# A two-layer hybrid diffusion backbone on one core: an output projection split into two passes, a product loop turned inside out, and tiles moved to other start addresses

## The chip, the cores and the metric

One core of a Trainium2 chip runs the whole program. The metric is device time in microseconds (us), lower is better; three runs of the kernel before are given, and a fourth execution was taken by the hardware profiler. All times below are from those.

## The reference, cut to what matters

```python
def diff_attend(q, k, v, lam):                       # layer 1, 8 heads of two 64-wide halves
    s = jnp.einsum('bqhd,bkhd->bhqk', q, k) * DIFF_SUB_DIM ** -0.5
    p = softmax(s).reshape(b, DIFF_HEADS, 2, lq, k.shape[1])
    a = p[:, :, 0] - lam * p[:, :, 1]
    return jnp.einsum('bhqk,bkhd->bqhd', a, v)
def finish(o):                                       # per-head RMS norm, then the output projection
    o = rms_norm(o, subln_w) * (1.0 - lam_init)
    return o.reshape(..., 8 * 128) @ w_out
x = layer_norm(ALPHA * x + gate * finish(o))         # then the feed-forward part
...
def neighbourhood_attention(...):                    # layer 0: local keys plus context keys, one softmax
    return einsum(p_loc, v_r) + einsum(p_ctx, v_ctx)
def conv_ffn(u, w_up, conv_w, conv_b, w_down):
    val, gate = split(dwconv_centred(u @ w_up, conv_w, conv_b), 2)
    return (silu(gate) * val) @ w_down
```

There are 512 latent and 256 context tokens, width 1024, feed-forward width 2816. Layer 0 has a state-space branch beside neighbourhood attention, layer 1 the differential attention, and each layer ends in a feed-forward part. All data are float32.

## The kernel before, in words

**Precision.** Dense products run in fp32r on pairs: each operand is split into hi and lo, and `PASS` (hi x hi, hi x lo, lo x hi) makes three matmuls of what is mathematically one. `wchunk` (L127) loads 128x1024 of weights into `raw` by SP's queue, optionally multiplies by a gate row on POOL (L146), makes `whi` on ACT (L147) and `wlo` on DVE or POOL (L148). There are two `raw` buffers and eight `w` buffers.

**Where tiles lie.** Left-hand pools follow one another: `cst` (L84) ends at byte 22,080 of a partition, which is 64 past a multiple of 128, and the buffers of `blk`, `rawp`, `arp` and `wf` behind it are multiples of 128 bytes long, so all of them start 64 past one. `blk` holds activations (`u`, `ux`, `dact`, `act`, residual rows `y`) and `wf` the weight pairs. Right-hand pools hang from byte 229,344, 96 past a multiple of 128: the feed-forward activations `fact`, the split attention outputs `att` and the neighbourhood tiles (`nQ`, `nKh`, `V`) start 96 past one. In the pool `dp` of the differential attention, `K`, `Qh` and `Ql` happen to start at multiples of 128.

**Order.** The program is written in source order; a planner at build time (L1440, with a timeline of its own) gives each engine and each DMA queue one fixed order, with source order as priority and its own estimate of when operands are ready. On the chip each queue runs in that order and waits at its head.

**Neighbourhood attention** (`na_unit`, L723): a unit handles 128 queries and two heads, e = 0 and 1. Scores go to PSUM, softmax to `P`, TensorE transposes `P`, `Pt` is the copy of it in SBUF (L759), and then the value products (L765 to L767) run over e outside and over key chunks inside: the head e uses columns 64e to 64e+63 of the array and the same partitions of the PSUM tile `av`. Four pairs of heads have four units with four chunks and two context units with two chunks each. These products are plain fp32, and each shows as two records in the trace. `run` (L801) interleaves these units with the state-space groups and dense products.

**Feed-forward** (`up` L994, `down` L1019): `fpx` (512 latent tokens) and `fpc` (context) have `whi`/`wlo` as stationary operand and `u` as moving one, at L300; `pdn` at L1032 has a 128-token slice of `fact` as stationary operand and 512 columns of the weight as moving one.

**Differential attention** (L1201 to L1325). For a head `d_qk` makes rotated keys and queries; `d_head` (L1201) runs four rounds of 128 queries: scores `dSp` (L1210), maximum, exponential (L1217), difference `dP` (L1222), six transposes `atp` (L1227), value products `avp` (L1231), copy to `ob` and sum of squares (L1233, L1234). After each round it takes one step of a generator `filler`. Heads 0 to 5 are stored to DRAM (`scrO`). `d_prep` (L1242) takes two heads: a Sqrt on ACT for the norm, `ob` loaded back by SP (L1257), scaled (L1258), transposed through PSUM (`otp`, L1262), and split into `dact` (L1263, L1264). `d_out` (L1268) loads the projection weights of its heads, and for each of four token tiles tt and two column halves sums 3 products per head in one PSUM tile of the ring `pmm` (two slots) and adds the sum to `Yt[tt]` on DVE (L330).

Heads 0 and 1 are projected as filler of head 6, heads 2 and 3 as filler of head 7, and heads 4 to 7 after head 7 in one `d_out` of 12 products per sum, whose sums are followed by layer norm (`bn_stats`, `ln_to_u` L344: normalise, transpose `lntp`, scale, split into `u5`) and, on POOL, `affine` (L372).

PSUM is full: `pm2` two slots (tag mm), `pax` two (tag ax, used by `atp`, `avp`), `pS` two of double size (tag S, for scores).

Of the kernel before, what the change touches and what calls it, by code (L numbers as in the profile page):

```python
# [74 lines left out]
def emit(tc, T):  # L75
# [8 lines left out]
    cst = enter(tc.tile_pool(name="cst", bufs=1))  # L84
    blk = enter(tc.tile_pool(name="blk", bufs=18))
# [637 lines left out]
    def na_unit(Q, Kh, Kl, V, qo, k0, chunks, bias, out, pool, tp_, nb):  # L723
# [39 lines left out]
        for e in range(2):  # L763
            hp = HALF[e]
            for i, c in enumerate(chunks):  # L765
                m = toks[c][1]
                nc.tensor.matmul(av[hp], V[0:m, c, hp], Ss[e][1][0:m, i], start=(i == 0), stop=(i == len(chunks) - 1))  # L767
# [209 lines left out]
    def ffn(l, u, Y, with_ctx, u_next, last, close, pieces=()):  # L977
# [4 lines left out]
        fcw = fR.tile([128, 2 * NF, 4], F32, name="fcw")  # L982
# [259 lines left out]
    def d_prep(h, obs=None):  # L1242
        r = rso[:, h:h + 2].rearrange("p a b -> p (a b)")
        s0 = ds0[:, h:h + 2].rearrange("p a b -> p (a b)")
        nc.vector.tensor_scalar(r, dss[:, h:h + 2].rearrange("p a b -> p (a b)"), 1.0 / 128, None, op0=OP.mult)
# [6 lines left out]
        for i in range(2):  # L1252
            if obs:
                ob = obs[i]
            else:
                ob = (blk if h else dp).tile([128, 4, 128], F32, name="ob", tag="b" if h else "ob", bufs=None if h else 3)
                nc.sync.dma_start(ob, scrO[h + i])  # L1257
            (nc.gpsimd if h + i in OB_POOL else nc.vector).tensor_tensor(ob, ob, rso[:, h + i].unsqueeze(2).to_broadcast([128, 4, 128]), op=OP.mult)  # L1258
            at_ = blk.tile([128, 2, 512], F32R, name="dact", tag="b")
            tp = (pax if h == 6 else pmm).tile([128, 512], F32, name="otp", tag="ax" if h == 6 else "mm")  # L1260
            for q in range(4):
                nc.tensor.transpose(tp[:, 128 * q:128 * q + 128], ob[:, q], ident)  # L1262
            nc.scalar.activation(at_[:, 0], tp, AF.Copy, scale=sublnw)  # L1263
            nc.vector.scalar_tensor_tensor(at_[:, 1], tp, sublnw, at_[:, 0].bitcast(F32), op0=OP.mult, op1=OP.subtract)  # L1264
            acts.append(at_)
        return acts

    def d_out(hs, acts, wr=W, last=False):  # L1268
# [3 lines left out]
        n = 3 * len(hs)  # L1272
        for tt in range(4):
            bs = new_stats(dp) if last else None
            for hf in range(2):
                ps = pmm.tile([128, 512], F32, name="dpo", tag="mm")
                m = 0
                for kt in range(len(hs)):
                    for wi, ui in PASS:
                        nc.tensor.matmul(ps, acts[kt][:, ui, 128 * tt:128 * tt + 128], ws[kt][wi][:, 0, 512 * hf:512 * hf + 512],  # L1280
                                         start=(m == 0), stop=(m == n - 1))
                        m += 1
                add_ps(Yt[tt], ps, 512 * hf, 512, bs[:, hf] if last else None)
            if last:
                ln_to_u(Yt[tt], bs, tt, u5, sc3, sh3, dp, pS, "S", "dP", 4, 2)
            yield
# [3 lines left out]
    obs = []  # L1290
    filler, acts = (), []
    for h in range(8):
# [4 lines left out]
        obs = obs[-1:] + [d_head(h, *qk, Vh, filler)]  # L1297
# [5 lines left out]
        if h == 6:  # L1303
            qn = qx
# [4 lines left out]
        if h == 2:  # L1309
            acts = d_prep(0)  # L1310
        if h == 5:
            filler = d_out((0, 1), acts)
        if h == 6:
            acts = d_prep(2)
            filler = d_out((2, 3), acts, (blk, "b"))
        if h == 7:
            acts = d_prep(4)
# [4 lines left out]
    for _ in d_out((4, 5, 6, 7), acts + d_prep(6, obs), W, True):  # L1322
        pass
# [120 lines left out]
```

## Time and profile before

| what | us |
|---|---|
| runs | 2042.38, 2033.87, 2041.36 (median 2041.36) |
| profiled execution, its own time | 2034.78 |
| its span, first to last instruction | 2033.0 |
| PE busy | 1937.5 (95%) |
| weight loads (PEld) | 1649.1 (81%) |
| DVE, ACT, POOL busy | 1383.6, 893.9, 752.2 |

The profiled execution is 6.6 us below the median of the runs and within their spread. A row of the profile gives a group of instructions by line, engine and tiles (out<-in), their number, the time in which any of them ran, the mean of one, and the idle time of the engine before them with what ended it. Matmuls are pipelined: the duration of one (some 0.39 us for 512 columns) overlaps the next, and the cost in a stream is the distance from start to start. In a timeline row, consecutive instructions of one group are merged (x2), so the distance of two rows is to be divided by the number in the first.

### The profile page before, as it was taken

To read this page: it belongs to the slowest core of one execution; us is meant where nothing else is said; L and a number is where in the kernel's file an instruction comes from. 1 tells how busy PE (TensorE), PEld (TensorE's weight loads), DVE (VectorE), ACT (ScalarE), POOL (GpSimd) and SP (SyncE) were. 2 spreads that over 40 slices of the span, in tenths; PEclk is the share of its full clock that TensorE was granted. 3 is DMA by queue.
4 is the path that set the end of the run, shared out by engine and by line. 5 is a ranking of instruction groups with operands and counts; after the bars stand their busy time and mean duration, and the time that the engine had idled before them with its cause. 6 is when DMAs were issued, how large, how long until landed. Compare 5 with 4: busy or idle time off the path is not lost. (4 is left out here: it accounts for less than half of the span.)

```text
span 2033.0 us, 31103 instructions
## 1 busy us (share of the span) xinstructions
PE 1937.5 (95%) x11928; PEld 1649.1 (81%) x11928; DVE 1383.6 (68%) x2202; ACT 893.9 (44%) x1756; POOL 752.2 (37%) x635
## 2 busy tenths in 40 slices
PE   7998999999999889999999999999999899999998
PEld 5887878897677788888888887898997688888886
DVE  3757566767567968978776658676665776655567
ACT  3545456675343532222222233556564544333332
POOL 2136225245226835344444428421124274222123
PEclk9999999999899999999999999999999999999999
DMA  9335332233422234334333331422112223322231
GB/s 312 121 105 172 99 123 89 81 131 122 148 93 84 96 114 135 124 113 138 116 124 103 104 104 42 138 64 74 63 55 65 88 77 112 104 87 100 89 108 62
DMA packets 109299, 217.58 MB, mean 107 GB/s; under 512 B 27096, under 2 KB 45888, under 8 KB 109152
## 3 DMA queue, kind: packets, MB, share of 16 engines
q1 hardware_dynamic: 98480, 189.44, 28.7%
q0 software_dynamic: 6016, 20.03, 2.9%
q10 hardware_dynamic: 4656, 6.13, 1.0%
q8 instruction: 94, 1.54, 0.3%
q14 instruction: 53, 0.43, 0.1%
HBM read 202.81 MB, written 8.55 MB: 104 GB/s over the span
## 5 line engine op out<-in xcount | busy, mean ns | idle before, releaser
L147 ACT ACTIVATE whi<-raw 128x1024 fp32r<-128x1024 f32 (+1 forms) x205 | 215.3, 1056 | 410.2 <-PE fpc L300 143.3
L148 DVE TENSOR_TENSOR wlo<-raw,whi 128x1024 fp32r<-128x1024 f32 (+1 forms) x192 | 258.2, 1349 | 159.1 <-ACT whi L147 156.1
L324 POOL TENSOR_TENSOR y<-y,ev 128x512 f32<-128x512 f32 x144 | 210.0, 1479 | 206.8 <-DVE ev L322 165.2
L1032 PE MATMUL pdn<-whi,fact 128*128 128x512 f32 x880 | 277.8, 397 | 3.3 <-DVE ev L322 2.3
L300 PE MATMUL fpx<-ux,whi 128*128 128x512 f32 (+1 forms) x832 | 232.3, 364 | 2.1 <-DVE cv L991 2.1
L300 PE MATMUL fpx<-u,whi 128*128 128x512 f32 (+1 forms) x832 | 227.7, 359 | 2.8 <-DVE cv L991 1.8
L1032 PEld LDWEIGHTS pdn<-whi,fact 128*128 128x128 f32 x880 | 163.1, 188 | 42.6 <-DVE ev L322 4.0
L1016 POOL TENSOR_TENSOR fact<-cv,fact 128x768 fp32r<-128x768 f32 (+1 forms) x44 | 73.9, 1679 | 269.1 <-ACT fact L1015 269.1
L1032 PE MATMUL pdn<-wlo,fact 128*128 128x512 f32 x440 | 172.3, 394 | 0.0
L300 PEld LDWEIGHTS fpx<-ux,whi 128*128 128x128 f32 x832 | 150.1, 193 | 25.8 <-issue 3.9
L300 PEld LDWEIGHTS fpx<-u,whi 128*128 128x128 f32 x832 | 149.3, 191 | 26.7 <-ACT cv L987 2.0
L300 PE MATMUL fpx<-ux,wlo 128*128 128x512 f32 (+1 forms) x416 | 151.7, 365 | 1.8 <-DVE wlo L148 1.8
L300 PE MATMUL fpx<-u,wlo 128*128 128x512 f32 (+1 forms) x416 | 149.3, 360 | 1.3 <-DVE wlo L148 1.3
L300 PE MATMUL px<-ux,whi 128*128 128x512 f32 x448 | 149.8, 406 | 0.7 <-ACT whi L147 0.7
L991 DVE SCALAR_TENSOR_TENSOR cv<-fpx,fcw,cv 128x511 f32<-128x511 f32 x176 | 130.5, 744 | 28.2 <-ACT cv L987 26.9
L193 DVE SCALAR_TENSOR_TENSOR acc<-araw,condp,acc 128x512 f32<-128x512 f32 x140 | 131.1, 958 | 22.9 <-DMA araw<-in_ada_w 22.4
L146 POOL TENSOR_TENSOR raw<-raw,G 128x1024 f32<-128x1024 f32 x30 | 73.9, 2467 | 176.0 <-DMA raw<-in_w_down 94.4
L300 PE MATMUL fpc<-uc,whi 128*128 128x256 f32 x704 | 130.3, 283 | 1.4 <-DVE uc L370 1.4
L300 PEld LDWEIGHTS fpc<-uc,whi 128*128 128x128 f32 x704 | 111.9, 191 | 6.0 <-DVE uc L370 1.6
L375 POOL TENSOR_TENSOR y<-y,gb 128x256 f32<-128x256 f32 x112 | 101.4, 940 | 32.0 <-PE lntp L354 32.0
L322 DVE SCALAR_TENSOR_TENSOR ev<-pdn,G 128x512 f32<-128x512 f32 x120 | 81.1, 681 | 32.0 <-POOL y L324 17.9
L987 ACT ACTIVATE cv<-fpx,fcw 128x512 f32<-128x512 f32 x88 | 67.6, 770 | 79.7 <-PE fpx L300 77.4
(330 smaller groups left out, 4632.5 us busy)
## 6 DMA issues: line engine op xcount, KB each, us to landing
araw<-in_ada_w SPq DMA_DIRECT2D x96, 512.0 KB
raw<-in_w_up SPq DMA_DIRECT2D x88, 512.0 KB
raw<-in_w_down SPq DMA_DIRECT2D x44, 512.0 KB
E<-scr POOLq DMA_DIRECT2D x24, 512.0 KB, 5.0
raw<-in_w_dqk SPq DMA_DIRECT2D x16, 512.0 KB
raw<-in_w_qkv SPq DMA_DIRECT2D x12, 512.0 KB
raw<-in_w_out SPq DMA_DIRECT2D x12, 512.0 KB
raw<-in_w_bc SPq DMA_DIRECT2D x8, 512.0 KB
```

The source lines that it names most:

```text
L146: nc.gpsimd.tensor_tensor(raw, raw, gate, op=OP.mult)
L147: nc.scalar.activation(hi[:, :n], raw[:, :n], AF.Copy)
L148: (eng or nc.vector).tensor_tensor(lo[:, :n], raw[:, :n], hi[:, :n].bitcast(F32), op=OP.subtract)
L193: nc.vector.scalar_tensor_tensor(acc[:, s], raw[:, i], cs, acc[:, s], op0=OP.mult, op1=OP.add)
L300: nc.tensor.matmul(ps, w[wi][:, kc], rhs(kc, ui), start=(i == 0), stop=(i == n - 1))
L322: nc.vector.scalar_tensor_tensor(t, ps, r, Gh, op0=OP.mult, op1=OP.mult)
L324: eng.tensor_tensor(yh, yh, t, op=OP.add)
L375: nc.gpsimd.tensor_tensor(y[:, c:c + 256], y[:, c:c + 256], t[:, c:c + 256], op=op)
L987: nc.scalar.activation(dst, src, AF.Identity, bias=f[:, 3:4], scale=f[:, 1:2])
L991: nc.vector.scalar_tensor_tensor(dst[:, lo:hi_], src[:, lo + d:hi_ + d], f[:, tap:tap + 1], dst[:, lo:hi_], op0=OP.mult, op1=OP.add)
L1016: nc.gpsimd.tensor_tensor(at_[:, 1], val, at_[:, 0].bitcast(F32), op=OP.subtract)
L1032: nc.tensor.matmul(ps, acts[2 * gs[0] + kt][:, ui, 128 * tt:128 * tt + 128], ws[kt][wi][:, 0, o:o + 512], start=(m == 0), stop=(m == 3 * n ...
```

## The change

It adds a 64-byte pad to `cst` and a 96-byte pool at the right-hand end, written once by POOL, and makes `fcw` 64 bytes longer. In `na_unit` the loops over e and over chunks change places. Of the differential attention, `d_prep` takes any number of heads and gets loaded `ob` tiles; the weight loads become a function of their own (`do_w`), called for heads 0 and 1 ahead of head 6 and for heads 2 to 7 after it; heads 4, 5 and 6 are prepared after head 6, ahead of head 7. The last projection holds four accumulators (two of `pm2`, two of `pax`): 9 products of heads 4 to 6 for each of two token tiles and two halves, then the preparation of head 7 (its transposes through `pS`), then 3 products of head 7 for each, with sums and layer norm; then the same for the other two token tiles.

```diff
--- before.py
+++ after.py
@@ -82,6 +82,10 @@
         return bass.AP(tensor=t.tensor, offset=t.offset + off, ap=[[0, parts], [1, n]])
 
     cst = enter(tc.tile_pool(name="cst", bufs=1))
+
+    end = enter(tc.tile_pool(name="end", bufs=1, side=RIGHT))
+    for pool, n in ((cst, 16), (end, 24)):
+        nc.gpsimd.memset(pool.tile([128, n], F32, name="pad"), 0.0)
     blk = enter(tc.tile_pool(name="blk", bufs=18))
     rawp = enter(tc.tile_pool(name="rawp", bufs=2))
     arp = enter(tc.tile_pool(name="arp", bufs=2))
@@ -760,10 +764,10 @@
                 i = j
             Ss.append((S, Pt))
         av = Ss[0][0][:, 0:128]
-        for e in range(2):
-            hp = HALF[e]
-            for i, c in enumerate(chunks):
-                m = toks[c][1]
+        for i, c in enumerate(chunks):
+            m = toks[c][1]
+            for e in range(2):
+                hp = HALF[e]
                 nc.tensor.matmul(av[hp], V[0:m, c, hp], Ss[e][1][0:m, i], start=(i == 0), stop=(i == len(chunks) - 1))
         out(av)
 
@@ -979,7 +983,7 @@
         sR = ExitStack()
         fR = sR.enter_context(tc.tile_pool(name=f"fR{l}", bufs=1, side=RIGHT))
         acts = {}
-        fcw = fR.tile([128, 2 * NF, 4], F32, name="fcw")
+        fcw = fR.tile([128, 2 * NF + 4, 4], F32, name="fcw")[:, 0:2 * NF]
         nc.sync.dma_start(fcw, T["fcw"][:, l])
 
         def conv3(ci, src, m, dst):
@@ -1239,25 +1243,26 @@
             nc.scalar.dma_start(scrO[h], ob)
         return ob
 
-    def d_prep(h, obs=None):
-        r = rso[:, h:h + 2].rearrange("p a b -> p (a b)")
-        s0 = ds0[:, h:h + 2].rearrange("p a b -> p (a b)")
-        nc.vector.tensor_scalar(r, dss[:, h:h + 2].rearrange("p a b -> p (a b)"), 1.0 / 128, None, op0=OP.mult)
+    def d_load(h, first):
+        ob = (dp if first else blk).tile([128, 4, 128], F32, name="ob", tag="ob" if first else "b", bufs=3 if first else None)
+        nc.sync.dma_start(ob, scrO[h])
+        return ob
+
+    def d_prep(h, obs, pool=None, tag="mm"):
+        m = len(obs)
+        r = rso[:, h:h + m].rearrange("p a b -> p (a b)")
+        s0 = ds0[:, h:h + m].rearrange("p a b -> p (a b)")
+        nc.vector.tensor_scalar(r, dss[:, h:h + m].rearrange("p a b -> p (a b)"), 1.0 / 128, None, op0=OP.mult)
         nc.vector.tensor_tensor(s0, s0, s0, op=OP.mult)
         nc.vector.scalar_tensor_tensor(r, s0, RMS_EPS, r, op0=OP.mult, op1=OP.add)
         nc.scalar.activation(r, r, AF.Sqrt)
         nc.vector.reciprocal(r, r)
         nc.vector.tensor_scalar(r, r, 1.0 - LAM_INIT, None, op0=OP.mult)
         acts = []
-        for i in range(2):
-            if obs:
-                ob = obs[i]
-            else:
-                ob = (blk if h else dp).tile([128, 4, 128], F32, name="ob", tag="b" if h else "ob", bufs=None if h else 3)
-                nc.sync.dma_start(ob, scrO[h + i])
+        for i, ob in enumerate(obs):
             (nc.gpsimd if h + i in OB_POOL else nc.vector).tensor_tensor(ob, ob, rso[:, h + i].unsqueeze(2).to_broadcast([128, 4, 128]), op=OP.mult)
             at_ = blk.tile([128, 2, 512], F32R, name="dact", tag="b")
-            tp = (pax if h == 6 else pmm).tile([128, 512], F32, name="otp", tag="ax" if h == 6 else "mm")
+            tp = (pool or pmm).tile([128, 512], F32, name="otp", tag=tag)
             for q in range(4):
                 nc.tensor.transpose(tp[:, 128 * q:128 * q + 128], ob[:, q], ident)
             nc.scalar.activation(at_[:, 0], tp, AF.Copy, scale=sublnw)
@@ -1265,62 +1270,75 @@
             acts.append(at_)
         return acts
 
-    def d_out(hs, acts, wr=W, last=False):
+    def do_w(hs, wr=W):
         wring[:] = [wr]
         ws = [wchunk(T["w_do"][h], (1, 1024), G, nc.gpsimd if h in DO_POOL else None) for h in hs]
         wring[:] = [W]
-        n = 3 * len(hs)
+        return ws
+
+    def do_mm(ps, tt, hf, acts, ws, first=True, last=True):
+        n = 3 * len(ws)
+        m = 0
+        for at_, w in zip(acts, ws):
+            for wi, ui in PASS:
+                nc.tensor.matmul(ps, at_[:, ui, 128 * tt:128 * tt + 128], w[wi][:, 0, 512 * hf:512 * hf + 512],
+                                 start=(first and m == 0), stop=(last and m == n - 1))
+                m += 1
+
+    def d_out(acts, ws):
         for tt in range(4):
-            bs = new_stats(dp) if last else None
             for hf in range(2):
                 ps = pmm.tile([128, 512], F32, name="dpo", tag="mm")
-                m = 0
-                for kt in range(len(hs)):
-                    for wi, ui in PASS:
-                        nc.tensor.matmul(ps, acts[kt][:, ui, 128 * tt:128 * tt + 128], ws[kt][wi][:, 0, 512 * hf:512 * hf + 512],
-                                         start=(m == 0), stop=(m == n - 1))
-                        m += 1
-                add_ps(Yt[tt], ps, 512 * hf, 512, bs[:, hf] if last else None)
-            if last:
-                ln_to_u(Yt[tt], bs, tt, u5, sc3, sh3, dp, pS, "S", "dP", 4, 2)
+                do_mm(ps, tt, hf, acts, ws)
+                add_ps(Yt[tt], ps, 512 * hf, 512, None)
             yield
 
     scrO = drp.tile([8, 128, 4, 128], F32, name="scrO")
     qn = d_qk(0)
-    obs = []
     filler, acts = (), []
     for h in range(8):
         Vh = V
         qk = qn
         if h == 6:
             qx = d_qk(7)
-        obs = obs[-1:] + [d_head(h, *qk, Vh, filler)]
+            filler = d_out(acts, do_w((0, 1)))
+        ob = d_head(h, *qk, Vh, filler)
         if h < 6:
             qn = d_qk(h + 1)
             if h % 2 == 0:
                 gv = d_v(h // 2 + 1)
             Vn = take(gv, 3)
-        if h == 6:
-            qn = qx
         if h % 2 == 1:
             V = Vn
         if h == 2:
             G = gate_rows(1, 0, 0, arp, "ar")
-        if h == 2:
-            acts = d_prep(0)
-        if h == 5:
-            filler = d_out((0, 1), acts)
+            acts = d_prep(0, [d_load(0, True), d_load(1, False)])
         if h == 6:
-            acts = d_prep(2)
-            filler = d_out((2, 3), acts, (blk, "b"))
-        if h == 7:
-            acts = d_prep(4)
+            qn = qx
+            acts = d_prep(2, [d_load(2, False), d_load(3, False)])
+            filler = d_out(acts, do_w((2, 3), (blk, "b")))
+            wl = do_w((4, 5, 6, 7))
+            acts = d_prep(4, [d_load(4, False), d_load(5, False), ob])
     gb = gb_rows(1, 0, blk, "b")
     sc3, sh3 = mod_params(1, 1)
     fold_ln(1, 0, sc3, sh3)
     u5 = ([blk.tile([128, 2, 512], F32R, name="u5", tag="b") for k in range(KC)], None)
-    for _ in d_out((4, 5, 6, 7), acts + d_prep(6, obs), W, True):
-        pass
+
+    po4 = Ring((pm2, "mm"), (pm2, "mm"), (pax, "ax"), (pax, "ax"))
+    for t2 in range(2):
+        pss_ = {}
+        for tt in (2 * t2, 2 * t2 + 1):
+            for hf in range(2):
+                ps = pss_[tt, hf] = po4.tile([128, 512], F32, name="dpo", tag=None)
+                do_mm(ps, tt, hf, acts, wl[:3], last=False)
+        if t2 == 0:
+            acts7 = d_prep(7, [ob], pS, "S")
+        for tt in (2 * t2, 2 * t2 + 1):
+            bs = new_stats(dp)
+            for hf in range(2):
+                do_mm(pss_[tt, hf], tt, hf, acts7, wl[3:], first=False)
+                add_ps(Yt[tt], pss_[tt, hf], 512 * hf, 512, bs[:, hf])
+            ln_to_u(Yt[tt], bs, tt, u5, sc3, sh3, dp, pS, "S", "dP", 4, 2)
     for tt in range(4):
         affine(Yt[tt], gb)
     s7.close()
```

## Rows read from the trace of the kernel before

**Rows 1.** The page, parts 1 and 2: busy time, granted clock in 40 slices.

```profile
PE 1937.5 (95%) x11928; PEld 1649.1 (81%) x11928; DVE 1383.6 (68%) x2202; ACT 893.9 (44%) x1756; POOL 752.2 (37%) x635
...
PEclk9999999999899999999999999999999999999999
```

**Rows 2.** Stretches: length, then PE, PEld, DVE, ACT, POOL busy; clock, DMA.

```profile
200.00:300.00 100.00, 98.93 (x706) 81.24 (x705) 56.22 (x124) 50.13 (x111) 22.86 (x32) 1.00 0.36 110
...
730.00:1270.00 540.00, 531.26 (x2906) 446.26 (x2904) 411.19 (x555) 160.34 (x232) 239.04 (x162) 1.00 0.34 110
...
1600.00:1620.00 20.00, 13.46 (x80) 11.16 (x79) 12.77 (x15) 7.47 (x19) 6.08 (x4) 0.91 0.39 146
...
1640.00:1660.00 20.00, 16.73 (x105) 14.30 (x104) 19.59 (x34) 11.01 (x26) 18.03 (x20) 1.00 0.15 53
```

**Rows 3.** Groups of TensorE by shape: xcount | busy us, mean ns.

```profile
L1032 PE MATMUL pdn<-whi,fact 128*128 128x512 f32 x880 | 277.8, 397 | 3.3 <-DVE ev L322 2.3 <-ACT whi L147 1.0
...
L300 PE MATMUL fpx<-u,whi 128*128 128x512 f32 x576 | 179.4, 390 | 0.0
L1032 PE MATMUL pdn<-wlo,fact 128*128 128x512 f32 x440 | 172.3, 394 | 0.0
...
L300 PE MATMUL fpc<-uc,whi 128*128 128x256 f32 x704 | 130.3, 283 | 1.4 <-DVE uc L370 1.4
```

**Rows 4.** Timeline of TensorE in the second feed-forward part: `pdn`, then `fpx`.

```profile
1744.25 0.63 PE L1032 MATMUL pdn<-whi,fact 128*128 128x512 f32 x2
...
1748.45 0.40 PE L300 MATMUL fpx<-u,wlo 128*128 128x512 f32 x1
...
1788.05 0.62 PE L300 MATMUL fpx<-u,whi 128*128 128x512 f32 x2
...
1789.42 0.61 PE L300 MATMUL fpx<-u,whi 128*128 128x512 f32 x2
```

**Rows 5.** The same view: scores of a differential head; 256-column `fpx`.

```profile
1564.62 0.39 PE L1210 MATMUL dSp<-K,Qh 128*128 128x512 f32 x1
...
1565.32 0.39 PE L1210 MATMUL dSp<-K,Qh 128*128 128x512 f32 x1
...
1654.21 0.40 PE L300 MATMUL fpx<-u,whi 128*128 128x256 f32 x2
...
1654.57 0.52 PE L300 MATMUL fpx<-u,whi 128*128 128x256 f32 x3
```

**Rows 6.** The same view: value products of neighbourhood units (L767).

```profile
435.76 0.66 PE L767 MATMUL S<-Pt,V 128*64 128x128 f32 x8
...
512.69 1.09 PE L767 MATMUL S<-Pt,V 128*64 128x128 f32 x8
516.35 1.09 PE L767 MATMUL S<-Pt,V 128*64 128x128 f32 x8
```

**Rows 7.** L767 by line: records in all, and waits before them.

```profile
L767 PE MATMUL S<-Pt,V x320: 269/273/476, 233.4 to 617.2; 128*64 128x128 f32 x144, 64*64 64x128 f32 x16
...
  ACT Pt L759: 3.8, 7
```

**Rows 8.** Timeline of TensorE at the end of the differential attention: waits in brackets.

```profile
1604.86 0.73 PE L1280 MATMUL dpo<-whi,dact 128*128 128x512 f32 x2 [1.56 <-DVE y L330]
...
1615.31 1.11 PE L1262 MATMUL otp<-c_consts,ob 128*128 128x128 f32 x4 [4.19 <-DVE ob L1258]
...
1623.14 1.23 PE L1262 MATMUL otp<-c_consts,ob 128*128 128x128 f32 x8 [1.56 <-DVE ob L1258]
```

**Rows 9.** Timelines of SP, ACT and DVE there.

```profile
1607.99 0.38 SPq L1257 DMA_DIRECT2D ob<-scrO  x1
...
1620.33 1.28 ACT L1248 ACT_TABLE_LOAD   x1
...
1628.85 1.29 DVE L330 TENSOR_TENSOR y<-y,dpo 128x512 f32<-128x512 f32 x2 [2.91 <-PE dpo L1280]
```

**Rows 10.** Timeline of POOL at the start of the program.

```profile
18.72 3.10 POOL L417 TENSOR_SCALAR xraw<-xraw,sc,sh 128x256 f32<-128x256 f32 x2 [18.27 <-ACT uc L415]
```

## The prediction, made before the changed kernel was run

> **What bounds the kernel now.** I read the page first: TensorE (PE) is busy 95% of the span, DVE 68%, and the granted clock is at its upper level nearly everywhere [rows 1]. The stretches come next: in 200 to 300 us PE works 98.93 of 100 us, and in the long run of the feed-forward part 531.26 of 540 [rows 2]. So in most of the program only a cheaper TensorE instruction gives time; a faster DVE, ACT or DMA gives none there. The end of the differential attention is different: from 1600 to 1620 PE works 13.46 of 20 us at a clock of 0.91, and from 1640 to 1660 DVE is the full one, 19.59 of 20 [rows 2]. The change touches both kinds, so its three parts are costed apart, against the profiled execution's own time of 2034.8 us, which is 6.6 us below the median of the runs.
>
> **Part one, the aligned tiles.** The pad moves `blk` and `wf` (so `u`, `ux`, `whi`, `wlo`) from 64 past a multiple of 128 to 0, and the pool at the other end moves `fact`, `att` and the neighbourhood tiles from 96 past to 0. What a start address is worth must come from streams that differ in it. `pdn` has its stationary operand at 96 and its moving one at 64; from 1744.25 to 1748.45 eighteen products start, 4.20 us, 0.2333 each [rows 4]. `fpx` has both at 64: 1.37 us for six, 0.2283 each [rows 4]. So 96 against 64 costs 5.0 ns, which the mean durations repeat, 397 and 394 ns against 390 [rows 3]. For 0 against 64 the scores `dSp` are the nearest row, since `K` and `Qh` start at 0: from 1564.62 to 1565.32 two 512-column and two 256-column products start, 0.70 us [rows 5]; `fpx` and `fpc` prices for the same are 2 x 0.2283 + 2 x 0.120 (three 256-column products in 0.36 us) = 0.697 [rows 4, 5]. So 0 is no better than 64, and only the users of the tiles at 96 gain. There are 880 + 440 `pdn` products [rows 3], and 1,320 x 5.0 ns = 6.6 us, which all lie on the bounding engine. **I take -6.6.** The bounds: 0 if the 5 ns has another cause (`pdn` changes its stationary operand with every product, as `fpx` does, but its two streams come from other pools), and a loss of as much, +6.6, since `K` and `Qh` now go to 64 and nothing shows what a mixed pair costs.
>
> The rule that speaks against this part is in the Trainium skill, SBUF — State Buffer, Specifications (TRN2): lines of SBUF are 16 bytes. By it 64 and 96 are as good as 0, and this term would be 0. The trace differs between 96 and 64 [rows 4], so it speaks against that reading by 5 ns a product, not more.
>
> Two pads are written by POOL, which waits 18.27 us for its first data [rows 10]: no cost as long as it idles there, and some 0.5 us at worst on an engine off the path.
>
> **Part two, the value products alternate.** There are 320 records for 160 products [rows 7]. Eight records of one head take 1.09 us, and eight of a context unit, which hold one change of head in the middle, 0.66 [rows 6]. The two heads use different columns of the array, so records of different heads overlap. Were all records at 1.09 per eight now and at 0.66 then, 40 x 0.43 = 17.2 us would go. Not all are: the context units and the middle of every pair already overlap. I take a third, rounded down, **-5**; the bounds are -17 and 0. Against it stands a wait: all of e = 0's products could so far run ahead of e = 1's softmax; now the second product waits for e = 1's `Pt`, and in PE's fixed order everything behind it waits as well. Today `Pt` costs PE 3.8 us in seven waits [rows 7]. In most units both heads' products stand together in the timeline, so nothing new waits; at 512.69 and 516.35 they are 3.66 us apart [rows 6]. That is the second rival.
>
> **Part three, the last projection.** PE's waits between 1600 and 1625 that belong to it are 1.56 (`y`), 4.19 (`ob`) and 1.56 (`ob`) [rows 8], 7.3 us. The 4.19 is a load: head 5's `ob` is issued by SP at 1607.99 [rows 9] and its transposes run at 1615.31 [rows 8]. With heads 4 to 6 prepared ahead of head 7's rounds that load and its wait lie beside these rounds. The last wait is head 7's preparation, from ACT's table load at 1620.33 [rows 9] to the end of the transposes about 5 us later; now 36 products of heads 4 to 6, 36 x 0.2283 = 8.2 us, stand in front of it and cover it. So PE's waits go. But the end is not PE's: DVE is full from 1640 to 1660 [rows 2], so time is gained only as far as the first sum of the last pass comes earlier. It starts at 1628.85 now, after 2.91 us of waiting [rows 9]. Then it must wait for one full set of 36 products and the first three of head 7, 39 x 0.2283 = 8.9 us behind the last value products, instead of the preparation and twelve products. That is about the same distance as now; what is left is the 4.19 us that lay ahead, and about 1 us more of the order of sums. **I take -5.** What is added: a Sqrt and then again an exponential between heads 6 and 7, two table loads of 1.28 us on ACT [rows 9], covered by the 48 products of heads 2 and 3, 11 us, that run as filler there; three `ob` loads that SP issues behind six weight loads instead of four; and one PSUM ring of four that also serves the transposes and value products of the last round. Bounds: -9.1 (all 7.3 and the clock back, 0.09 of 20 us = 1.8), and +8.3 where the load's wait of 4.19, two table loads and one more preparation of 1.56 show instead of being covered. If the cover goes, the next thing late is head 7's first `dP`, whose exponential stands behind Sqrt on ACT.
>
> The weight loads in a function of their own issue the same 8 chunks; the pieces of SP's and POOL's queues that come earlier are those of heads 2 to 7, and POOL, 37% busy [rows 1], has room in that stretch. I cost them at nothing; without that room each is one of the waits in the +8.3.
>
> **Sum:** -6.6 - 5 - 5 = -16.6, and 2034.8 - 16.6 = 2018.2. The median of the runs shown lies 6.6 above, so the same sum against it gives 2024.8; I give **2020**, nearer the profiled one.
>
> **The rivals.**
> *Starts don't matter.* Then only -5 and -5 are left, 2024.8. For it: `dSp` shows 0 as good as 64 [rows 5]. Against it: 397 against 390 ns over 880 and 576 records [rows 3]. Chance 0.17.
>
> *Starts matter much more.* If a pair at 0 and 0 ran without any gap, at 512/2.4 = 213 ns, `pdn` would give 1,320 x 20 = 26 us and the 576 `fpx` of one group 576 x 15 = 9, the 704 `fpc` 704 x 13 = 9, and the other groups of `fpx` and layer-0 products about as much again, some 80 us: 2034.8 - 80 - 10 = about 1945. The scores at 0 and 0 speak against it [rows 5]. Chance 0.06.
>
> *Slower: PE waits for the second head.* If e = 1's `Pt` is as late in each of the 24 units as at 512.69, e = 0's 1.09 us can no longer run before it: 24 x 1.09 = 26 us more, against -6.6 and -5: 2034.8 + 26 - 11.6 = about 2049. It decides once idle time before these products for `Pt` goes from 3.8 to over 20 us. Most units show both heads' records in one piece, against it. Chance 0.07.
>
> *The tail gives nothing.* New waits of up to 8.3 us as above, with the two other parts: 2034.8 + 8.3 - 11.6 = 2031.5, no change. For it: DVE is the full engine there [rows 2]. Chance 0.13.
>
> **How the numbers follow.** The forecast has 0.57, its own range about 2005 to 2030 (the bounds of the three terms taken half way). The range that holds 8 in 10 reaches down to **1990** (the value products' whole 17 and more of the alignment) and up to **2040**, which takes in the first and last rival and leaves out the one near 1945 and the slower one. About 0.5%, 10 us, is what a measurement can tell from no change. Faster by more: most of the forecast (0.50), a bit over half of the first rival (0.10), all of the second (0.06) and a little of the last (0.04), **0.70**. Slower: the third rival and a remnant of the last, **0.09**. Within: **0.21**.
>
> **What would show it.** Alignment: `pdn`'s mean goes from 397 to about 390, its distance to 0.228, while `fpx` stays at 390 and `dSp` as it is; if `fpx` falls too, my reading of 0 against 64 is wrong. Value products: sixteen records in 1.4 us or less, `Pt` waits below 10 us. Tail: no wait of over 1 us for `ob`, the first sum of the last pass some 4 us nearer to the start of head 7, DVE full behind it. The prediction is wrong where none of the three terms is found, or where waits for `Pt` or ACT's tables stand in their place.

## The result, and the profile after

The changed kernel is slower: 2052.73 us median of 14 runs against 2036.88 of 14 runs of the kernel before, a ratio of 1.0069 with a 95% interval of 1.0059 to 1.0080. (The ratios of this document are worked out from all runs of both kernels; the quotient of two medians can differ from them, here it is 1.0078.) It was forecast faster, at 2020, within 1990 to 2040. The profiled execution took 2055.46 us, its span is 2053.7.

The page of the changed kernel, parts 1 and 2:

```profile
PE 1937.4 (94%) x11928; PEld 1660.9 (81%) x11928; DVE 1382.8 (67%) x2202; ACT 899.3 (44%) x1758; POOL 748.0 (36%) x637
...
PEclk9999999998889999999999999999999999999999
```

TensorE (PE) is as busy as before, to 0.1 us of 1937 [rows 1], although `pdn` and the value products now cost less; so the 20.7 us between the two spans (2053.7 and 2033.0) are idle time of PE, and what the cheaper products save is lost again in products that take longer: the mean granted clock of the span is 0.971 in place of 0.984. Where the time lies is read from the first and the last start of a few groups. By tile, the kernel before (count: minimum/median/maximum ns, first to last start):

```profile
L300 PE MATMUL fpx<-ux,whi x832: 278/389/629, 674.1 to 1212.8; 128*128 128x512 f32 x115, 128*128 128x256 f32 x52
...
L1210 PE MATMUL dSp<-K,Qh x128: 277/376/500, 1327.1 to 1598.1; 128*128 128x512 f32 x64, 128*128 128x256 f32 x64
...
L1231 PE MATMUL avp<-dV,At x384: 270/275/377, 1346.6 to 1619.5; 128*128 128x128 f32 x192
...
L1280 PE MATMUL dpo<-wlo,dact x64: 386/390/628, 1552.1 to 1647.6; 128*128 128x512 f32 x64
...
L300 PE MATMUL fpx<-u,whi x832: 274/389/416, 1649.8 to 1989.8; 128*128 128x512 f32 x115, 128*128 128x256 f32 x52
...
L1032 PE MATMUL pdn<-wlo,fact x440: 388/392/497, 762.1 to 2023.7; 128*128 128x512 f32 x147
```

The same, and the value products with their wait for `Pt` (as in [rows 7], of PE and of its weight loads together), of the changed kernel (its lines stand 4 to 6 further down):

```profile
L771 PE MATMUL S<-Pt,V x320: 269/273/478, 237.3 to 637.8; 128*64 128x128 f32 x144, 64*64 64x128 f32 x16
...
  ACT Pt L763: 4.1, 6
...
L304 PE MATMUL fpx<-ux,whi x832: 274/389/628, 691.8 to 1230.9; 128*128 128x512 f32 x115, 128*128 128x256 f32 x52
...
L1214 PE MATMUL dSp<-K,Qh x128: 274/390/792, 1345.4 to 1613.2; 128*128 128x512 f32 x64, 128*128 128x256 f32 x64
...
L1235 PE MATMUL avp<-dV,At x384: 270/275/497, 1364.5 to 1628.0; 128*128 128x128 f32 x192
...
L1284 PE MATMUL dpo<-wlo,dact x64: 388/389/400, 1569.4 to 1659.7; 128*128 128x512 f32 x64
...
L304 PE MATMUL fpx<-u,whi x832: 279/389/583, 1668.1 to 2011.2; 128*128 128x512 f32 x115, 128*128 128x256 f32 x52
...
L1036 PE MATMUL pdn<-wlo,fact x440: 387/389/500, 780.5 to 2044.1; 128*128 128x512 f32 x147
```

| from start to start | before | after | difference |
|---|---|---|---|
| start of the span to first value product | 233.4 | 237.3 | +3.9 |
| first to last value product | 383.8 | 400.5 | +16.7 |
| last value product to first `fpx` of layer 0 | 56.9 | 54.0 | -2.9 |
| first `fpx` to first `dSp` | 653.0 | 653.6 | +0.6 |
| first `dSp` to last `avp` | 292.4 | 282.6 | -9.8 |
| last `avp` to last `dpo` | 28.1 | 31.7 | +3.6 |
| last `dpo` to first `fpx` of layer 1 | 2.2 | 8.4 | +6.2 |
| first `fpx` of layer 1 to last `pdn` | 373.9 | 376.0 | +2.1 |
| last `pdn` to the end of the span | 9.3 | 9.6 | +0.3 |

(383.8 is 617.2 - 233.4 [rows 7]. Value products are those of neighbourhood attention; `avp` are those of the differential attention.) Most of the loss lies in neighbourhood attention; around the last projection 9.8 us are won ahead of the last `avp` and given back between it and the first `fpx` of layer 1. The stretches of the changed kernel in neighbourhood attention (length, then PE, PEld, DVE, ACT and POOL busy, clock, DMA):

```profile
450.00:500.00 50.00, 46.44 (x275) 39.61 (x274) 27.92 (x61) 30.22 (x80) 22.33 (x29) 0.94 0.37 119
500.00:550.00 50.00, 37.41 (x188) 29.09 (x187) 29.76 (x67) 18.76 (x52) 12.56 (x17) 0.82 0.50 169
550.00:600.00 50.00, 42.65 (x192) 30.18 (x190) 25.11 (x47) 21.14 (x53) 12.76 (x8) 0.83 0.24 75
```

and of the kernel before:

```profile
450.00:500.00 50.00, 50.00 (x317) 42.27 (x316) 30.36 (x64) 27.59 (x76) 23.54 (x29) 1.00 0.36 122
500.00:550.00 50.00, 40.26 (x194) 29.87 (x193) 35.33 (x78) 25.28 (x67) 17.06 (x19) 0.83 0.48 168
550.00:600.00 50.00, 49.65 (x258) 38.02 (x257) 27.34 (x54) 20.31 (x55) 12.57 (x9) 1.00 0.24 75
```

From 450 to 600 PE is busy 126.5 us in place of 139.9. Between 550 and 600 the clock is 0.83 instead of 1.00, so about a third of it ((1 - 0.83) / 0.5) ran at 1.2 GHz in place of 2.4, behind a stretch in which PE was busy 37.41 of 50 us. The wait for `Pt`, by which the slower rival was to be recognised, has not grown: 4.1 us in 6 waits against 3.8 in 7 [rows 7].

### The profile page after: what moved, and what is told of

Same layout as the page of the kernel before. It is cut to its first block, busy times and chain, and to the rows that moved or that the text cites. A ratio compares the mean times of both kernels' runs of the same rounds, so it can differ in the third digit from the quotient of the medians.

```text
span 2053.7 us, 31113 instructions
## 1 busy us (share of the span) xinstructions
PE 1937.4 (94%) x11928; PEld 1660.9 (81%) x11928; DVE 1382.8 (67%) x2202; ACT 899.3 (44%) x1758; POOL 748.0 (36%) x637
## 5 line engine op out<-in xcount | busy, mean ns | idle before, releaser
L151 ACT ACTIVATE whi<-raw 128x1024 fp32r<-128x1024 f32 (+1 forms) x205 | 215.2, 1056 | 412.8 <-PE fpc L304 139.9
L1036 PE MATMUL pdn<-whi,fact 128*128 128x512 f32 x880 | 272.3, 391 | 4.5 <-DVE ev L326 3.4
```

Source lines behind the costliest of these rows:

```text
L151: nc.scalar.activation(hi[:, :n], raw[:, :n], AF.Copy)
L1036: nc.tensor.matmul(ps, acts[2 * gs[0] + kt][:, ui, 128 * tt:128 * tt + 128], ws[kt][wi][:, 0, o:o + 512], start=(m == 0), stop=(m == 3 * n ...
```

## The experiments

### The parts one at a time

e1 has the two pads and the longer `fcw` alone, e2 the exchanged loops alone, e3 the new last projection alone, e4 the change without the exchanged loops. Each edit is that part of the diff of the change; for e2 it is

```diff
-        for e in range(2):
-            hp = HALF[e]
-            for i, c in enumerate(chunks):
-                m = toks[c][1]
+        for i, c in enumerate(chunks):
+            m = toks[c][1]
+            for e in range(2):
+                hp = HALF[e]
```

> The kernel before with the two pads and the longer fcw alone; the order of every engine's instructions is that of before. Theory (a start 96 past a multiple of 128 costs pdn 5 ns): pdn's mean falls from 397 to about 390 ns, the time by 6.6 us, ratio about 0.997. Rival (starts cost nothing, the 5 ns has another cause): pdn stays at 397, ratio 1.000. Second rival (a start at 0 gains over 64 as well): fpx falls below 390 and the time by 40 us or more, ratio under 0.98.

> The kernel before with the loops over heads and chunks of the value products exchanged, nothing else. Theory from the trace of the change, whose last value product starts 20.6 us later than before: this part alone loses most of that, so the last value product is 15 to 20 us late and the ratio is 1.007 to 1.010. Rival (the loss comes from the start addresses or from the profiled execution alone): the products overlap, -5 us, ratio about 0.9975.

> The kernel before with the new last projection alone. Theory (as predicted: the waits for ob go): -5 us, ratio about 0.9975. Rival from the trace of the change, where the last value product of the differential attention gains about 10 us on its first score and the first fpx of layer 1 loses them again: 0 us, ratio 1.000, with the time moved from waits ahead of the last value product into waits behind it.

> The changed kernel with the value products in the order of before: pads and new last projection together. Theory (the exchanged loops are the whole loss, the other parts keep their sign): about 2036.9 - 6.6 - 5 = 2025, ratio 0.994. Rival (the last projection gives nothing): 2030, ratio 0.997. Rival (the loss is in the pads or the last projection): ratio over 1.003.

| run | median us | ratio | 95% interval |
|---|---|---|---|
| e1, pads | 2033.45 | 0.9961 | 0.9947 to 0.9974 |
| e2, exchanged loops | 2051.29 | 1.0061 | 1.0049 to 1.0074 |
| e3, last projection | 2044.24 | 1.0027 | 1.0015 to 1.0039 |
| e4, pads and last projection | 2039.12 | 0.9994 | 0.9985 to 1.0003 |

Of the 2038.80 us that the kernel before took beside them, these ratios are -8, +12.5 and +5.5 us for the three parts, in sum +10 of the change's +14. The pads gain about what was expected (by the interval of e1 5 to 11 us), the two other parts lose. For e3 neither the theory (-5) nor its rival (0) came out. e4 is about the sum of its parts, -8 + 5.5; its theory, that only the loops lose, falls, and both its rivals with it. e2 loses as its theory said, a little less than the 1.007 to 1.010 expected. Its value products run from 236.1 to 639.8 us, so the last one is 22.6 us late, and they wait for `Pt` as little as before, in its rows by line:

```profile
L767 PE MATMUL S<-Pt,V x320: 269/273/477, 236.1 to 639.8; 128*64 128x128 f32 x144, 64*64 64x128 f32 x16
...
  ACT Pt L759: 3.7, 6
```

### The exchanged loops: products or order?

The program is ordered by a planner that works from source order and its own estimates. The pads leave every engine's order as it was. The exchanged loops do not: from the first unit on, other instructions of PE, DVE, ACT, POOL and SP change places too. e5 and e6 separate the two. A list of the instructions of PE, DVE, ACT and POOL up to the second layer, in the planned order of one kernel, is given to the other as constraints:

```diff
+        for a, b in zip(order, order[1:]):
+            if a >= 0 and b >= 0:
+                tc.add_manual_dep(made[b], made[a].name, ..., reason="issue order")
```

> Alternating value products alone, as in e2, but every engine's instructions up to the second layer are pinned to the order that the planner made for the kernel before; of each unit the alternating products stand where the second head's products stood. Theory (the new order that the planner made loses the 12.5 us of e2, the products cost nothing): the last value product is back at 610 to 620 us, ratio 0.997 to 1.001. Rival (the alternating products themselves lose, by the wait for the second head): ratio 1.005 or more.

> The kernel before, value products by heads as before, but every engine's instructions pinned to the order that the planner made for e2. Theory (the order loses): as slow as e2, ratio 1.005 to 1.008, last value product at 635 to 640 us. Rival (the products lose): ratio 0.999 to 1.002.

| | planned order of before | planned order of e2 |
|---|---|---|
| products by heads | 1 | e6: 1.0100 (1.0086 to 1.0115) |
| products alternate | e5: 0.9941 (0.9929 to 0.9954) | e2: 1.0061 (1.0049 to 1.0074) |

The alternating products gain 12 us where nothing else moves but one copy of `Pt`, which the planner gave to DVE in place of ACT (2028.89 against 2040.37), and 8 us in the new order (1.0100 to 1.0061). The new order alone costs 20 us, with the products as they always were, and 24 us with alternating products (0.9941 to 1.0061). Both runs lie outside what was expected of them: e5 was to gain nothing (0.997 to 1.001), e6 to lose less (1.005 to 1.008). In e5, the value products by line:

```profile
L769 PE MATMUL S<-Pt,V x320: 269/273/476, 236.1 to 610.8; 128*64 128x128 f32 x144, 64*64 64x128 f32 x16
...
```

One unit in the timeline of the kernel before, both heads in one piece, and the same unit in e5:

```profile
272.99 1.58 PE L767 MATMUL S<-Pt,V 128*64 128x128 f32 x16
```

```profile
273.61 1.09 PE L769 MATMUL S<-Pt,V 128*64 128x128 f32 x16
```

Sixteen records take 1.09 us in place of 1.58, as long as eight of one head alone [rows 6]. All value products together keep PE busy for 26.0 us in e5 and 41.5 in the kernel before, and from the first to the last of them PE is busy 359.8 us in place of 372.2. Those 12.4 us are the gain of e5: the products are cheaper by themselves. In the changed kernel the planner issues one product as soon as the first head is ready and the others when the second is; its timeline:

```profile
527.67 0.43 PE L771 MATMUL S<-Pt,V 128*64 128x128 f32 x2
...
532.81 1.09 PE L771 MATMUL S<-Pt,V 128*64 128x128 f32 x14
```

What the new order does is seen, for one, at the transposes `ytp`, which stand among the later units. By tile, what PE waited for before them, in the kernel before and in the changed one:

```profile
  DVE act L838: 0.2, 1
```

```profile
  DVE act L842: 5.8, 3
  DMA yr<-scrY: 3.1, 1
```

PE stands at the head of its queue for `act` and `yr`, 8.9 us in four waits instead of 0.2 in one, and what stands behind waits as well. The same holds for the units' own softmax: by tile `S`, PE's wait for `P` ahead of the transposes of `P` in the kernel before and in the changed one:

```profile
  DVE P L746: 1.7, 1
```

```profile
  DVE P L750: 6.3, 2
```

The wait for `nQ` ahead of the scores goes from 0.4 to 4.6 us. e6, whose products are those of the kernel before, shows the same waits, and its value products end at 640.2:

```profile
L769 PE MATMUL S<-Pt,V x320: 269/273/476, 234.4 to 640.2; 128*64 128x128 f32 x144, 64*64 64x128 f32 x16
```

```profile
  DVE act L840: 5.6, 2
  DMA yr<-scrY: 2.8, 1
```

Its waits for `P` and `nQ` are 6.5 and 4.6 us. From its first to its last value product e6 takes 405.8 us in place of 383.8, which is about its whole loss: PE is idle there for 24.5 us in place of 11.6, and for the same products it is busy 381.3 us in place of 372.2, at a mean granted clock of 0.96 in place of 0.98. So some 13 us are waits, for `P`, `nQ`, `act` and `yr` above all, and some 9 us go with the lower clock. Which moved instruction of DVE or ACT makes each of these operands late was not taken apart.

### The last projection

e3 leaves the order of layer 0 as it was. In it the projections of heads 2 and 3 no longer run beside head 7's rounds. DVE's timeline of e3: the last sum of heads 0 and 1, the scale factors of heads 4 to 6, and the first two sums of heads 2 and 3.

```profile
1578.21 0.68 DVE L330 TENSOR_TENSOR y<-y,dpo 128x512 f32<-128x512 f32 x1
...
1607.18 0.17 DVE L1256 TENSOR_SCALAR rso<-rso 128x12 f32<-128x12 f32 x1
...
1617.90 0.69 DVE L330 TENSOR_TENSOR y<-y,dpo 128x512 f32<-128x512 f32 x1
...
1622.35 0.68 DVE L330 TENSOR_TENSOR y<-y,dpo 128x512 f32<-128x512 f32 x1
```

Nothing is summed for 39 us. The preparation of heads 4 to 6 stands ahead of head 7 in source order, so by the kernel's order its transposes `otp` take the two slots of `pmm` before the first product of heads 2 and 3 does, and they wait for the norm of head 6. (The products could also be late for their place behind `otp` in PE's queue; no run separates the two.) From the first `dSp` to the first `fpx` of layer 1, e3 still takes no longer than the kernel before, 322.2 us against 322.7. It is the stretch from there to the last `pdn` that is 6.1 us longer, 379.9 against 373.9: PE waits there 5.5 us for the next weights of the feed-forward part, and the mean granted clock of the stretch is 0.982 in place of 0.995.

```profile
1694.18 1.35 PE L300 MATMUL fpx<-u,whi 128*128 128x256 f32 x4 [5.51 <-ACT whi L147]
```

The changed kernel has the same wait, 5.87 us; in its table the cheaper `pdn` hides part of what it costs. e7 moves the preparation into the last filler step:

```diff
+    def then(steps, obs):
+        for i, _ in enumerate(steps):
+            if i == 3:
+                acts4.extend(d_prep(4, obs))
+            yield
...
-            filler = d_out(acts, do_w((2, 3), (blk, "b")))
+            filler = then(d_out(acts, do_w((2, 3), (blk, "b"))), [d_load(4, False), d_load(5, False), ob])
             wl = do_w((4, 5, 6, 7))
-            acts = d_prep(4, [d_load(4, False), d_load(5, False), ob])
```

e8 does this as well, and takes only token tiles 0 and 1 in four accumulators, tiles 2 and 3 one after the other:

```diff
-    for t2 in range(2):
+    for tts in ((0, 1), (2,), (3,)):
...
                 do_mm(ps, tt, hf, acts, wl[:3], last=False)
+                if tt > 1:
+                    do_mm(ps, tt, hf, acts7, wl[3:], first=False)
```

> The new last projection alone, as in e3, but heads 4 to 6 are prepared in the last filler step of head 7 instead of ahead of head 7. Theory (their transposes take PSUM slots in front of the products of heads 2 and 3, which so fall out of head 7's rounds to behind them): the sums of heads 2 and 3 on DVE come between 1585 and 1610 us again and the 5.5 us of e3 are gone, ratio 0.996 to 1.000. Rival (the loss of e3 lies behind the last product, in layer norms that end together): ratio 1.002 to 1.004.

> As e7, and the last two token tiles are summed one after the other with all 12 products of a sum in one go, as in the kernel before; only the first two use four accumulators. Theory (in e3 the sums of two tiles end within three microseconds, and their two layer norms stand bare behind the last product): first fpx of layer 1 comes 3 to 5 us sooner behind the last dpo than in e7, ratio 0.994 to 0.998. Rival (the gap behind the last product is one layer norm and stays): the ratio of e7.

e7 gives 2038.92 us, 0.9992 (0.9981 to 1.0003): the loss of e3 is gone, 0.0035 or 7 us, and so is the wait for those weights. The sums of heads 2 and 3 are back in head 7's rounds, from 1586.17 us on:

```profile
1586.17 0.69 DVE L330 TENSOR_TENSOR y<-y,dpo 128x512 f32<-128x512 f32 x1 [0.21 <-PE dpo L1280]
```

e8 gives 2038.55 us, 0.9998 (0.9987 to 1.0009), no better than e7, and its first `fpx` of layer 1 comes 12.0 us behind the last `dpo` against 10.2 in e7: its theory falls. Part of why the repaired projection does not gain either is read from the layer norms. Their normalising step on DVE in the kernel before, four token tiles, and in e7, the first two of four:

```profile
1632.23 1.00 DVE L350 TENSOR_SCALAR y<-y,mv,rsy 128x512 f32<-128x512 f32 x2
...
1640.21 1.94 DVE L350 TENSOR_SCALAR y<-y,mv,rsy 128x512 f32<-128x512 f32 x2
...
1646.32 1.69 DVE L350 TENSOR_SCALAR y<-y,mv,rsy 128x512 f32<-128x512 f32 x2
...
1659.20 1.65 DVE L350 TENSOR_SCALAR y<-y,mv,rsy 128x512 f32<-128x512 f32 x2
```

```profile
1635.95 1.00 DVE L350 TENSOR_SCALAR y<-y,mv,rsy 128x512 f32<-128x512 f32 x2
...
1637.52 0.99 DVE L350 TENSOR_SCALAR y<-y,mv,rsy 128x512 f32<-128x512 f32 x2
```

Before, each token tile's norm lies beside the products of the next, and only the last one begins behind the last product (1647.6). With four accumulators two tiles end together: in e7 the two other norms begin at 1643.1 and 1655.1, both behind the last product (1640.4). PE's waits there, in e7:

```profile
1645.42 0.66 PE L354 MATMUL lntp<-c_consts,y 128*128 128x128 f32 x4 [3.79 <-DVE uf L362]
...
1650.61 1.22 PE L300 MATMUL fpx<-u,whi 128*128 128x256 f32 x4 [3.47 <-ACT u L367]
```

In the kernel before, the largest wait between the last `dpo` and the first `fpx` is 0.95 us. The two waits are most of what e7's first `fpx` loses behind the last `dpo`, 8.0 us (10.2 against 2.2). They do not take back everything: from the first `dSp` to the first `fpx` e7 takes 316.4 us, 6.3 less than the kernel before. What becomes of those is seen only in part. In e10 (below), which has the same projection, the stretch from the first `fpx` to the last `pdn` is 4.3 us longer than in e11 with the old one (373.0 against 368.7), 2.5 us of it in a longer wait for `cv`; the rest is open. e8 undoes only half of the pairing; whether norms placed as before would keep the gain was not tried.

### All together

e9 is the whole change in the old order, e10 the same with the preparation moved as in e7, e11 pads and alternating products with the old projection. Their edits are those of e5, e7 and e1.

> The whole change, with every engine's instructions up to the second layer pinned to the order of the kernel before, as in e5. Theory (three parts that add up: pads 0.9961, alternating products in the old order 0.9941, last projection 1.0027): ratio 0.993, 0.991 to 0.995. Rival (the pinned order and the pads do not add, since with faster products another wait ends last): ratio 0.996 or more.

> As e9, but with heads 4 to 6 prepared in the last filler step of head 7, as in e7. Theory (0.9961 x 0.9941 x 0.9992): ratio 0.989, 0.987 to 0.992, faster than both kernels. Rival (the last projection's loss was only hidden in e7's spread): the ratio of e9.

> Pads and alternating products in the old order, the last projection of the kernel before. Theory (the new last projection gives nothing even when repaired): ratio 0.990, within 0.002 of e10. Rival (it gives the 5 us that were predicted once nothing else hides it): slower than e10 by 0.002 or more.

| run | median us | ratio | 95% interval |
|---|---|---|---|
| e9 | 2029.11 | 0.9952 | 0.9937 to 0.9967 |
| e10 | 2022.20 | 0.9919 | 0.9906 to 0.9932 |
| e11 | 2024.13 | 0.9929 | 0.9916 to 0.9942 |

The same change is 1.0069 in the planner's new order and 0.9952 in the old one: the order costs it 1.2%, 24 us. e10 beats both kernels, by some 17 and 30 us. e11 lies within 0.0010 of it, so the new projection adds nothing that these runs can tell, as its theory said. The factors do not quite multiply: e11 should be 0.9961 x 0.9941 = 0.9902 and is 0.9929, a gain smaller by 5 us, and e9 should be 0.993 and is 0.9952, between its theory and its rival. The intervals of the parts allow for most of this; whether more is behind it stays open.

### Which start address counts

e12 leaves out the left pad, e13 and e14 put 32 and 64 bytes at the left alone, e15 32 bytes at the right alone. The order of the engines is that of before in all four. The starts follow from where the kernel puts its tiles; no trace shows an address. For e13 the edit is

```diff
     cst = enter(tc.tile_pool(name="cst", bufs=1))
+    nc.gpsimd.memset(cst.tile([128, 8], F32, name="pad"), 0.0)
```

> The kernel before with the 96 bytes at the right-hand end and the longer fcw, but without the 64 bytes in the first pool: fact and its neighbours go from 96 past a multiple of 128 to 0, while u, ux, whi and wlo stay at 64. Order of all engines as before. Theory (only the operand at 96 costs): pdn's mean 390 to 392 ns and the ratio of e1, 0.995 to 0.998. Rival (both operands must start at 0): pdn stays near 397, ratio 0.999 to 1.001.

> The kernel before with 32 bytes more at the end of the first pool and nothing at the right: u, ux, whi and wlo go from 64 to 96 past a multiple of 128, where fact lies already. Order of all engines as before. Theory from e12 (a product costs 4 to 6 ns more when its two operands start at different places within 128 bytes, wherever that is): pdn's mean falls from 397 to 390 to 392 ns, fpx stays at 390, ratio 0.995 to 0.998, as in e1. Rival (both operands must start at a multiple of 64 or 128): pdn stays near 397 and fpx rises above 393, ratio 1.002 or more.

> The kernel before with 64 bytes more at the end of the first pool and nothing at the right: the moving operand of pdn at 0, fact still at 96. Theory (the two starts must agree): pdn stays at 395 to 398 ns, ratio 0.998 to 1.002. Rival (the moving operand's start decides): pdn 390 to 392 ns, ratio 0.995 to 0.998.

> The kernel before with 32 bytes at the right-hand end and nothing else: fact goes from 96 to 64 past a multiple of 128, where u, ux, whi and wlo lie already; order as before. e13 (both at 96) left pdn at 396 ns, against the reading that two agreeing starts are enough. Theory A (only a multiple of 128 for both helps pdn): pdn stays at 395 to 398 ns, ratio 0.998 to 1.001. Theory B (agreeing starts help at multiples of 64): pdn 390 to 392 ns, ratio 0.995 to 0.998, and so 32 bytes do what the change does with 160.

`pdn` by shape (count, busy us and mean ns) in e1, with an `fpx` row beside it:

```profile
L1036 PE MATMUL pdn<-whi,fact 128*128 128x512 f32 x880 | 272.3, 391 | 4.9 <-DVE ev L326 3.8 <-ACT whi L151 1.0
...
L304 PE MATMUL fpx<-u,whi 128*128 128x512 f32 x576 | 178.5, 389 | 0.0
...
L1036 PE MATMUL pdn<-wlo,fact 128*128 128x512 f32 x440 | 170.9, 391 | 0.0
```

The `wlo` row of `pdn` in e12, e13, e14 and e15, in this order (their `whi` rows have means of 397, 396, 397 and 396):

```profile
L1035 PE MATMUL pdn<-wlo,fact 128*128 128x512 f32 x440 | 173.5, 396 | 0.0
```

```profile
L1033 PE MATMUL pdn<-wlo,fact 128*128 128x512 f32 x440 | 173.1, 396 | 0.0
```

```profile
L1033 PE MATMUL pdn<-wlo,fact 128*128 128x512 f32 x440 | 173.8, 397 | 0.0
```

```profile
L1035 PE MATMUL pdn<-wlo,fact 128*128 128x512 f32 x440 | 173.1, 396 | 0.0
```

| run | moving, stationary operand of `pdn`, bytes past a multiple of 128 | ratio | 95% interval |
|---|---|---|---|
| before | 64, 96 | 1 | |
| e1 | 0, 0 | 0.9961 | 0.9947 to 0.9974 |
| e12 | 64, 0 | 0.9991 | 0.9981 to 1.0002 |
| e13 | 96, 96 | 0.9988 | 0.9974 to 1.0002 |
| e14 | 0, 96 | 0.9993 | 0.9980 to 1.0007 |
| e15 | 64, 64 | 0.9997 | 0.9981 to 1.0013 |

The busy time of all 1,320 `pdn` goes from 450.1 us before to 443.2 in e1, -6.9, and is 449.5 to 451.5 in the four others. Of six pairs only the one with both at 0 makes `pdn` cheaper. Three readings fell one after the other: that the start at 96 is the dear one (e12), that the two must agree (e13), and that a common multiple of 64 is enough (e15). e14 came out as its theory said, and shows that the moving operand's start alone does nothing either.

## Why the prediction was wrong, point by point

**The aligned tiles** were sized rightly: -6.6 against -8 (e1), and `pdn` went to 391, about the 390 that the prediction's last part asked for. The step's reason failed: "0 is no better than 64, and only the users of the tiles at 96 gain". It was read from the scores, whose starts the pads later moved to 64 without a change, and from `fpx`; `pdn` itself gains nothing at 64 and 64 (e15), only at 0 and 0. The pads are one step of two halves, and each half alone is worth 0.0009 or less, which the runs cannot tell from nothing. That the right size came from a wrong reason is luck. The Trainium skill, SBUF — State Buffer, Specifications (TRN2), with its lines of 16 bytes, makes all six pairs equal; that agrees with layer 1's `fpx` (`fpx<-u`), whose mean stays at 389 to 390 ns with both operands at 0, 64 or 96, and not with `pdn` in e1.

**The value products** were sized too small: -5 was a third of the bound of -17, and e5 measures -12. The step that failed is one that the sum takes without saying so: that every other instruction stays in its place. The description of the kernel says that a planner orders the queues from source order and estimates, yet the only price given to the exchange is the products' own and a wait for `Pt`. The measured price is the reshuffled order, +20 us with the old products (e6) and +24 with the alternating ones, which turned -12 (e5) into +12.5 (e2).

**The slower rival** came out near the measured time (2049 against 2052.73) for another reason. Its sign to look for, idle time for `Pt` beyond 20 us, did not appear: 4.1 us. That sign was itself misread: the 3.8 us in seven waits [rows 7] count the waits of the weight loads with those of PE. PE alone waits 1.0 us for `Pt` in the kernel before and 1.5 in the changed one. The planner puts other work in front of the late products, and PE's waits grow elsewhere, by 13 us in all (e6), above all those for `P`, `nQ`, `act` and `yr`. That the time came out near 2049 is luck.

**The last projection**: -5 against +5.5 (e3), inside the bounds, and the range's +8.3 was meant for just such a case. The step that failed is the cover: the new preparation between heads 6 and 7, with its two table loads, was "covered by the 48 products of heads 2 and 3, 11 us, that run as filler there". But those 48 products stand behind the preparation and so left head 7's rounds (7 us, e3 against e7). The 9.8 us that the changed kernel saves ahead of the last `avp` are not the waits that went: 138 `dpo` stand behind it in place of 92, so 46 products by 0.2283 us, 10.5 us, moved from there. A wait for which the sum has no term comes on top: the 5.5 to 5.9 us for the feed-forward part's weights stand in e3, e4, e9 and the changed kernel, and are gone in e7. The second miss is in "DVE is full", named as the bound and not followed to its end: the gain was computed at the first sum, and the norms of two tiles that end together were not. The first sum did not come 4 us nearer to the start of head 7 either: it starts 51.6 us behind head 7's first score (1642.5 against 1590.9), before it was 50.8 (1628.85 against 1578.0).

**The rival "the tail gives nothing"** was right about this part: new waits of up to 8.3 us in e3, and no gain that the runs can tell once they are repaired (e7, e8, e10 against e11). **The rival "starts don't matter"** falls with e1, and **"starts matter much more"** with it, since `fpx` stays where it was.

## What to carry to other kernels

Where a planner fixes the order of the queues, a local edit has two effects, its own and the new order's. Compare the order of all engines before pricing anything, and pin it to measure the edit: here -12 us of edit came out as +12.5. Work that is moved ahead of a filler can take the filler's buffers as well as its place, so look which slots it claims, in which order, and what it waits for while it holds them.

## What the runs showed of the hardware

`pdn`, 512 columns in fp32r, costs 391 ns in the mean with both operands at a multiple of 128 bytes, and 396 to 397, over both of its groups, at the five other pairs of starts tried (e12 to e15 and the kernel before), while layer 1's `fpx` of the same shape stays at 389 to 390 at starts 0, 64 and 96. What sets `pdn` apart is open. Products on the two halves of the array's columns, issued in turn, took 1.09 us for sixteen records (e5), as long as eight on one half (the kernel before).
